# A two-layer fp32 trunk on one core: 32 bytes less padding ahead of the stages' pools, and steps of the attention plan in other places

## The chip, the cores and the metric

The kernel runs on one core of one Trainium2 chip. The metric is device time in microseconds (us), the median of three runs. A profile of one further execution gives a span (first to last instruction) and the trace that is read here. Engines: PE is TensorE's matmul, PEld its weight load, DVE is VectorE, ACT is ScalarE, POOL is GpSimd, SP issues DMAs.

## The reference, cut to what matters

512 positions, width 1024, two layers. Each layer is x + mixer(rmsnorm(x)) and then x + conv_ffn(rmsnorm(x)). The FFN is `(gelu(causal_dwconv(u)) * v) @ w_down` with `u, v = split(h @ w_up)` and 2816 hidden columns. The first layer's mixer is a causal pooling and a gated short convolution. The second layer's is the gated linear attention that the change touches:

```
q, k, v, r, gl = split(hn @ gla_w_in)
g    = log_sigmoid(gl @ w_g2 + b_g) / 16           # per head: cumulative sum bcum in chunks of 64
q_in = q * 128**-0.5 * exp(bcum);  k_in = k * exp(-bcum)
att  = where(tril, q_in @ k_in.T, 0);  kv = (k * exp(b_last - bcum)).T @ v
o    = att @ v + q_in @ states                     # states: decayed sum of kv over chunks
o    = o * rsqrt(mean(o*o) + eps) * norm_g * silu(r);   y = o @ gla_w_out
```

There are 4 heads, with 128 key columns and 256 value columns each.

## The kernel before, in words

All activations lie in SBUF transposed: 128 channels on partitions, 512 tokens along the free axis. A fp32 product is made of three fp32r matmuls: every operand is split into a high part (an ACT copy to fp32r, `high`) and a low part (a DVE subtraction, `low`), and high x high, high x low and low x high are summed in PSUM.

The large projections (w_up and the later part of w_down in both FFNs, and the query/key weights of the attention) are done by a seven-product scheme (`seven_weights`, line 473; `seven_product`, line 548): seven products p1 to p7 of 12 matmuls with 256 moving columns stand in for eight. There are 21 of them in each FFN's up part, 4 in each down part, and 4 in the attention (one for each head): 54 in all. A seven needs the weight parts a1, s31p, s2 and a2. Three of them have 1024 columns and lie in the ring `wsp` (tiles of `WPITCH` = 1088 columns, names `hi` and `lo`). s2 has 512 columns, serves product p6 alone, and lies in the pool of the stage (tiles of 576 columns, names `sh` and `sl`, line 509). All of them are put 19 columns (`SKEW`) into their tile. In the attention the products come in the order p1 p2 p6 p5 p7 p3 p4. p6, p7 and p4 go to the same PSUM bank as p1, one after another, so each must wait until an ACT copy (`keep`, line 1306) has fetched what stood there. p3 and p4 use a2.

Pools are opened in the order cp, big, wp, wsp, hp, sp and, last, the pool of the stage (`open_stage`: side, up, dn, up, gla and so on, one at a time); they lie in SBUF one behind another in this order. sp holds small tiles, each rounded up to 32 bytes a partition, and one tile "gap" that is never used (line 149). In the program's addresses cp to hp end at byte 201,600, a multiple of 128. sp takes 2,336 bytes, and every stage pool begins at byte 203,936, which is 32 past a multiple of 128. The `hi` and `lo` tiles begin at multiples of 128, and so do the activations (`xh`, `xl`, `th`, `tl`) that stream past the weights; the pitch of the `sh` and `sl` tiles (2,304 bytes) is a multiple of 128 too. In the stage dn the first three of the fourteen pairs `mh`, `ml` of the hidden activations that w_down's plain products stream lie in the stage's pool (`split_m`), the others in big.

The attention is written as a plan. `at(t, fn)` notes a step with a due time in us, `then` adds a PE step and moves the time on, and `run_plan` issues all steps in order of due time. On PE, DVE and ACT that order is kept as it stands, so an instruction waits for all that is planned ahead of it on its engine. DMAs go out on SP and POOL as their tiles come free. For each of four heads the plan has: a gate block r (`gate`, 24 matmuls of 512 columns, from a weight block whose high and low parts are due `split_at` us before it), the seven of query and key (`queries_keys`), three exponentials on ACT (`gates_of`: `decays2` makes exp(-b), line 1044; `decays` on DVE the difference and `decays3` the other two, lines 1048 and 1049), the keys on DVE (`head_keys`), `head_scores` (masked scores, and `key_rows` that copies the transposed keys), `head_kv` and `states`, `head_out`, the squares and the norm (`squares_of`, `head_norm`: two matmuls L311 and L312 need the ACT copy L315 and the DVE subtraction L316), and `out_gate` (times silu(r), and the split for the output projection `go`). Gate blocks 4 to 7 come after the fourth seven, and the last heads' pieces are put between their three parts.

Of the kernel before, what the change touches and what calls it, by code (L numbers as in the profile page):

```python
# [7 lines left out]
F32 = mybir.dt.float32  # L8
# [5 lines left out]
P = 128  # L14
# [58 lines left out]
def trunk_kernel(ctx, tc, xT, cols, w_ab, w_pool, w_abo, w_vg, w_qk, w_r, w_g2, w_go, w_up, w_dn, w_ds, outT):  # L73
# [72 lines left out]
    V.memset(ones, 1.0)  # L146
    ones_r = cp.tile([P, P], F32R, tag="ones_r", name="ones_r")
    V.tensor_copy(ones_r, ones)
    sp.tile([P, 56], F32, tag="gap", name="gap", bufs=1)
    warm_in = sp.tile([P, 1], F32, tag="warm", name="warm_in", bufs=1)  # L150
    S.activation(warm_in, ones[:, 0:1], AF.Abs_reciprocal_sqrt)
    warm = ps.tile([P, T], F32, tag="ps", name="warm")
# [306 lines left out]
    def at(t, fn):  # L459
        events.append((t, len(events), fn))  # L460
# [24 lines left out]
    def seven_weights(src, base, pool, sums, behind=None):  # L485
        w = {}

        def load_sum():
            s31 = w["s31"] = stage[pool].tile([P, WBLK], F32, tag="sum", name="s31", bufs=sums)
            part = src[:, None, D : D + QUARTER].broadcast_to([P, 2, QUARTER])  # L490
            nc.sync.dma_start(s31.rearrange("p (a n) -> p a n", a=2), part)

        def add_sum():
            part = src.rearrange("p (a n) -> p a n", a=4)[:, 0:4:3, :]
            G.dma_start(w["s31"].rearrange("p (a n) -> p a n", a=2), part, accum_op=ALU.add)  # L495

        def load_left():
            w["raw", 0] = wp.tile([P, WBLK], F32, tag="raw", name="raw")
            nc.sync.dma_start(w["raw", 0], src[:, :D])

        def load_right():
            w["raw", 1] = wp.tile([P, WBLK], F32, tag="raw", name="raw")
            nc.sync.dma_start(w["raw", 1][:, QUARTER:], src[:, D + QUARTER :])

        def tiles(kind, wide):
            if wide:
                return wsp.tile([P, WPITCH], F32R, tag=kind, name=kind)[:, SKEW : SKEW + WBLK]
            tag, bufs = "s" + kind[0], 2 if pool == "up" else 1
            return stage[pool].tile([P, T + 64], F32R, tag=tag, name=tag, bufs=bufs)[:, SKEW : SKEW + T]

        def high(name, src, wide=True):
            h = tiles("hi", wide)
            S.activation(h, src(), AF.Copy)  # L513
            w[name] = (h, src)

        def low(name, wide=True):
            h, src = w[name]
            lo = tiles("lo", wide)
            V.tensor_tensor(lo, src(), f32(h), ALU.subtract)  # L519
            w[name] = (h, lo)  # L520

        def s2_sum():
            s2 = w["raw", 1][:, :QUARTER]
            V.scalar_tensor_tensor(
                s2, w["s31"][:, QUARTER:], -1.0, w["raw", 0][:, :QUARTER], ALU.mult, ALU.subtract
            )

        def s4_sum():
            s2 = w["raw", 1][:, :QUARTER]
            V.tensor_tensor(s2, w["raw", 0][:, QUARTER:], s2, ALU.subtract)  # L530

        def queued_sum():
            with tc.issue_after(behind):
                load_sum()

        at(base - 26.0, queued_sum if behind else load_sum)
        at(base - 20.0, add_sum)
        at(base - 15.4, load_left)
        at(base - 9.7, load_right)
        at(base - 6.75, lambda: high("a1", lambda: w["raw", 0]))  # L540
        at(base - 4.35, lambda: low("a1"))
        at(base - 2.7, lambda: high("s31p", lambda: w["s31"]))
        at(base - 2.4, s2_sum)
        at(base - 1.65, lambda: high("s2", lambda: w["raw", 1][:, :QUARTER], False))
        at(base - 0.95, lambda: low("s2", False))
        at(base - 0.3, s4_sum)
        at(base + (0.4 if pool == "up" else 1.55), lambda: high("a2", lambda: w["raw", 1]))
        at(base + 1.5, lambda: low("s31p"))
        at(base + 3.3, lambda: low("a2"))

        return w

# [333 lines left out]
    rs, norm = norm_wide(acc, D)  # L886
# [155 lines left out]
    def decays2(h):  # L1042
        enb = heads[h]["enb"] = slot(name="enb")
        S.activation(enb, heads[h]["bc"], AF.Exp, scale=-1.0 / 16.0)
# [115 lines left out]
    def squares_of(h, t):  # L1160
        q = heads[h]

        def raw():
            q["sq"] = [slot(name="osq") for _ in range(2)]
            for sq, o in zip(q["sq"], q["o"]):
                S.activation(sq, o, AF.Square)

        def total():
            V.tensor_tensor(q["sq"][0], q["sq"][0], q["sq"][1], ALU.add)
            q["ro"], q["norm"] = norm_wide(q["sq"][0], 256, "ro")  # L1170

        at(t, raw)
        at(t + 1.3, total)
        ready_at = 6.5 if h < 2 else 1.7
        at(t + ready_at, lambda: q["norm"][0]())
        at(t + ready_at + 0.6, lambda: q["norm"][1]())

    def out_norm(h, t):
        q = heads[h]
# [10 lines left out]
    def out_gate(h, e, t):  # L1190
        i = 2 * h + e

        def gate():
            y = heads[h]["y"][e]
            V.tensor_tensor(y, y, sil[i], ALU.mult)

        def high():
            y_h[i] = slot(F32R, "yh")
            S.activation(y_h[i], heads[h]["y"][e], AF.Copy)

        def low():
            y_l[i] = slot(F32R, "yl")
            V.tensor_tensor(y_l[i], heads[h]["y"][e], f32(y_h[i]), ALU.subtract)

        at(t, gate)
        at(t + 0.8, high)
        at(t + 1.5, low)
# [12 lines left out]
    t = 0.0  # L1220
# [117 lines left out]
    def gate(i, between={}, split_at=(6.0, 4.8)):  # L1338
        project_into("r", i, store_r, between, split_at)
        at(t + 1.2, lambda: S.activation(sil[i], sil[i], AF.Silu))  # L1340
        sil_at[i] = t + 1.8
# [10 lines left out]
    def head_kv(h):  # L1352
        then(1.0, lambda: kv(h))
        at(t + 0.1, lambda: states(h))

    def head_out(h):
        then(3.1, lambda: outputs(h))
        squares_of(h, t + 0.1)

    def head_norm(h):  # L1360
        then(0.46, lambda: heads[h]["norm"][2]())
        out_norm(h, t + 0.1)
        scaled_at[h] = t + 5.4

    def gates_of(h, t):
        at(t + 2.0, lambda: decays(h))
        at(t + 3.0, lambda: decays2(h))
        at(t + 5.8, lambda: decays3(h))

    gate(0)  # L1370
    gates_of(0, t)
    queries_keys(0)
    head_keys(0, 1.6)
    gate(1, split_at=(4.6, 3.4))
    head_scores(0)
    gates_of(1, t)
    queries_keys(1)
    head_kv(0)
    head_keys(1, 1.6)
    gate(2, split_at=(4.6, 3.4))  # L1380
    head_out(0)
    head_scores(1)
    gates_of(2, t)
# [1 line left out]
    head_norm(0)  # L1385
    head_kv(1)
    head_keys(2, 1.6)
    gate(3, split_at=(4.6, 3.4))
    head_out(1)
    head_scores(2)  # L1390
    gates_of(3, t)
# [2 lines left out]
    head_norm(1)  # L1394
    head_kv(2)
    head_keys(3, 1.6)
    gate(4, split_at=(4.6, 3.4))
    head_out(2)
    head_scores(3)
    gate(5, {1: lambda: head_norm(2)})  # L1400
    head_kv(3)
    gate(6, {1: lambda: head_out(3)})
    gate(7, {1: lambda: head_norm(3)})
    for h in range(HEADS):
        for e in range(2):
            out_gate(h, e, max(scaled_at[h] + 0.7 * e, sil_at[2 * h + e], late + 10.0 * h + 0.7 * e if h < 2 else 0.0))
    for i in range(2):
        block(t - 8.0 + 3 * i, t - 5.0 + 2.5 * i, t - 3.8 + 2.5 * i)
    run_plan()
# [141 lines left out]
```

## Time and profile before

| | us |
|---|---|
| median of 3 runs (range) | 1017.31 (1017.26 to 1017.68) |
| the profiled execution: its own time | 1017.95 |
| its span | 1016.3 |
| PE busy | 1004.1 (99%) |
| DVE busy | 848.0 (83%) |
| ACT busy | 622.9 (61%) |
| mean granted TensorE clock | 0.996 of full speed |

In a timeline a row is a run of equal instructions: start, time from the first's start to the last's end, engine, line, operation, output <- inputs, count, and in brackets the idle time ahead of it with what ended it. Matmuls overlap, so the pace of PE is read from the differences between starts, not from the durations. The query/key products of head 0 begin at 524.86 us, those of head 3 at 585.64 us.

### The profile page before, as it was taken

What the parts mean: (1) busy time and instruction counts of PE and PEld (TensorE: products, weight loads), DVE (VectorE), ACT (ScalarE), POOL (GpSimd) and SP (SyncE); (2) the same over time, 40 slices, a digit from 0 to 9 for tenths busy, and PEclk for the clock granted to TensorE, in tenths of its full rate; (3) what the DMA queues carried; (4) which work ended last, traced back from release to release, by engine and by line L of the source; (5) the groups of instructions that cost most, each with busy time, mean ns of one, the idle gap of its engine ahead of it and who ended that gap; (6) DMA issues with size and microseconds to landing.
All of it is one profiled execution on the core that took longest, in us unless ns stands there. A gap on an engine that the chain in (4) does not pass through costs nothing.

```text
span 1016.3 us, 17534 instructions
## 1 busy us (share of the span) xinstructions
PE 1004.1 (99%) x6996; PEld 931.3 (92%) x6996; DVE 848.0 (83%) x1224; ACT 622.9 (61%) x954; POOL 69.6 (7%) x93
## 2 busy tenths in 40 slices
PE   9999999999999999999999999999999999999996
PEld 7888889999999988899999998889999999988896
DVE  7886689999999997767777788889999999997775
ACT  6442567676666754345775668767676666754451
POOL 0001000111111000002000000100110110000000
PEclk9999999999999999999999999999999999999998
DMA  6437137778787455527235122737778777454522
GB/s 226 153 92 185 56 102 186 181 196 191 187 203 183 132 129 143 129 76 203 90 96 132 53 63 84 194 107 192 172 199 187 194 199 191 127 130 131 130 83 84
DMA packets 61267, 147.03 MB, mean 145 GB/s; under 512 B 5152, under 2 KB 7584, under 8 KB 61184
## 3 DMA queue, kind: packets, MB, share of 16 engines
q1 hardware_dynamic: 45808, 116.93, 37.3%
q0 software_dynamic: 14688, 28.32, 17.1%
q8 instruction: 55, 0.90, 0.4%
q10 hardware_dynamic: 688, 0.65, 0.2%
q14 instruction: 28, 0.23, 0.1%
HBM read 143.78 MB, written 2.10 MB: 144 GB/s over the span
## 4 chain that ended last, share of the span: by engine, by line
PE 92%; DVE 4%; ACT 3%; issue 1%; DMA 1%; SPq 0%; DVEq 0%; ACTq 0%
PE stx L562 29%; PE styz L562 18%; PE dn L264 15%; PE go L264 4%; PE abo L264 4%; PE r L1274 3%; PE pc L264 2%; PE pb L264 2%; PE px L264 2%; PE dn L562 2%; PE stz L562 1%; PE v L596 1%; PE u L596 1%; PE pu L264 1%; PE vg L1065 1%
## 5 line engine op out<-in xcount | busy, mean ns | idle before, releaser
L519 DVE TENSOR_TENSOR lo<-raw,hi 128x1024 fp32r<-128x1024 f32 x108 | 131.7, 1220 | 12.9 <-ACT hi L513 12.9
L513 ACT ACTIVATE hi<-raw 128x1024 fp32r<-128x1024 f32 x108 | 114.1, 1057 | 21.5 <-PE styz L562 18.2
L223 DVE TENSOR_TENSOR lo<-raw,hi 128x1024 fp32r<-128x1024 f32 (+3 forms) x83 | 95.8, 1156 | 10.4 <-ACT hi L219 9.7
L219 ACT ACTIVATE hi<-raw 128x1024 fp32r<-128x1024 f32 (+3 forms) x83 | 83.1, 1001 | 19.2 <-PE pc L264 5.1
L495 POOL DMA_DIRECT2D s<-in_w_up x42 | 50.6, 1205 | 577.6 <-ACT k L614 102.3
L380 DVE SCALAR_TENSOR_TENSOR cacc<-u,colt,cacc 128x511 f32<-128x511 f32 x96 | 71.5, 745 | 1.8 <-ACT cacc L377 1.8
L377 ACT ACTIVATE cacc<-u,colt 128x512 f32<-128x512 f32 x48 | 39.2, 817 | 45.0 <-DVE u L629 35.9
L519 DVE TENSOR_TENSOR lo<-s,hi 128x1024 fp32r<-128x1024 f32 x54 | 65.7, 1216 | 0.0
L513 ACT ACTIVATE hi<-s 128x1024 fp32r<-128x1024 f32 x54 | 57.3, 1062 | 4.4
L562 PE MATMUL stx<-th,hi 128*128 128x256 f32 x368 | 56.9, 276 | 0.8 <-ACT q L1306 0.8
L264 PE MATMUL dn<-mh,hi 128*128 128x512 f32 (+1 forms) x238 | 57.0, 379 | 0.0
L264 PE MATMUL dn<-ml,hi 128*128 128x512 f32 (+1 forms) x238 | 56.9, 378 | 0.0
L264 PE MATMUL dn<-mh,lo 128*128 128x512 f32 (+1 forms) x238 | 56.8, 378 | 0.0
L562 PE MATMUL stx<-th,lo 128*128 128x256 f32 x368 | 56.8, 276 | 0.0
L562 PE MATMUL stx<-tl,hi 128*128 128x256 f32 x368 | 56.7, 276 | 0.0
L562 PE MATMUL styz<-xh,hi 128*128 128x256 f32 x360 | 55.8, 277 | 0.0
L562 PE MATMUL styz<-xh,lo 128*128 128x256 f32 x360 | 55.5, 276 | 0.0
L562 PE MATMUL styz<-xl,hi 128*128 128x256 f32 x360 | 55.4, 276 | 0.0
L264 PEld LDWEIGHTS dn<-mh,lo 128*128 128x128 f32 x238 | 43.0, 188 | 8.6
L264 PEld LDWEIGHTS dn<-ml,hi 128*128 128x128 f32 x238 | 43.0, 188 | 8.6
L264 PEld LDWEIGHTS dn<-mh,hi 128*128 128x128 f32 x238 | 42.3, 188 | 8.1
L562 PEld LDWEIGHTS stx<-th,hi 128*128 128x128 f32 x368 | 48.6, 188 | 1.0 <-ACT q L1306 1.0
(347 smaller groups left out, 2607.4 us busy)
## 6 DMA issues: line engine op xcount, KB each, us to landing
raw<-in_w_up SPq DMA_DIRECT2D x46, 512.0 KB, 6.0
s<-in_w_up SPq DMA_DIRECT2D x42, 512.0 KB, 6.8
s<-in_w_up POOLq DMA_DIRECT2D x42, 512.0 KB, 6.5
raw<-in_w_dn SPq DMA_DIRECT2D x32, 448.0 KB, 3.4
raw<-in_w_up SPq DMA_DIRECT2D x42, 256.0 KB, 3.3
raw<-in_w_ab SPq DMA_DIRECT2D x14, 512.0 KB, 3.7
raw<-in_w_abo SPq DMA_DIRECT2D x8, 512.0 KB, 4.1
s<-in_w_ds SPq DMA_DIRECT2D x8, 512.0 KB, 6.5
```

The source lines that it names most:

```text
L219: S.activation(parts[0], raw, AF.Copy)
L223: V.tensor_tensor(parts[1], raw, f32(parts[0]), ALU.subtract)
L264: PE.matmul(out, w[:, k, :], a[k], start=first and i == 0 and k == 0, stop=last and i == 2 and k == n - 1, skip_group_check=loose,)
L377: S.activation(acc[0], u, AF.Identity, bias=col(bname, j), scale=col(wname, 2 * nj + j))
L380: V.scalar_tensor_tensor(a, u[:, : T - i], col(wname, (2 - i) * nj + j), a, ALU.mult, ALU.add)
L495: G.dma_start(w["s31"].rearrange("p (a n) -> p a n", a=2), part, accum_op=ALU.add)
L513: S.activation(h, src(), AF.Copy)
L519: V.tensor_tensor(lo, src(), f32(h), ALU.subtract)
L562: PE.matmul(b[out][:, ts], wt[:, ks[k]], a[k], start=first and i == 0 and k == 0, stop=i == 2 and k == HK - 1, skip_group_check=True,)
L596: PE.matmul(o, w[:, k, :], a[k], start=i == 0 and k == 0, stop=i == 2 and k == KD - 1)
L1065: PE.matmul(o[c][:, :n], xh[kk][:, cs], lo[:, k, :], start=False, stop=kk == KD - 1)
L1274: PE.matmul(o, w[:, k, :], a[k], start=i == 0 and k == 0, stop=i == 2 and k == KD - 1, skip_group_check=True)
```

## The change

Every edit, with nothing left out:

```diff
-    sp.tile([P, 56], F32, tag="gap", name="gap", bufs=1)
+    sp.tile([P, 48], F32, tag="gap", name="gap", bufs=1)
...
-        at(base + (0.4 if pool == "up" else 1.55), lambda: high("a2", lambda: w["raw", 1]))
+        at(base + {"up": 0.4, "gla": 4.4}.get(pool, 1.55), lambda: high("a2", lambda: w["raw", 1]))
         at(base + 1.5, lambda: low("s31p"))
-        at(base + 3.3, lambda: low("a2"))
+        at(base + (5.3 if pool == "gla" else 3.3), lambda: low("a2"))
...
-        at(t + ready_at + 0.6, lambda: q["norm"][1]())
+        at(t + ready_at + (1.6 if h < 2 else 0.6), lambda: q["norm"][1]())
...
-        at(t + 3.0, lambda: decays2(h))
+        at(t + 1.6, lambda: decays2(h))
...
-    gate(1, split_at=(4.6, 3.4))
+    gate(1, split_at=(3.6, 2.4))          # gate(2), gate(3) and gate(4) alike
...
-    gate(5, {1: lambda: head_norm(2)})
-    head_kv(3)
-    gate(6, {1: lambda: head_out(3)})
+    gate(5, {1: lambda: (head_kv(3), head_norm(2))})
+    gate(6, {0: lambda: head_out(3)})
...
-            out_gate(h, e, max(scaled_at[h] + 0.7 * e, sil_at[2 * h + e], late + 10.0 * h + 0.7 * e if h < 2 else 0.0))
+            out_gate(h, e, max(scaled_at[h] + 0.7 * e, sil_at[2 * h + e], late + 5.0 + 8.0 * h + 0.7 * e if h < 2 else 0.0))
```

The gap tile has 8 columns fewer, so all that lies behind it, the stages' pools above all, moves down by 32 bytes: they begin at byte 203,904, a multiple of 128. In the attention, `high("a2")` is due 2.85 us later and `low("a2")` 2.0 us later; `decays2` comes 1.4 us earlier (in the order of ACT it passes from behind `high("a2")` to ahead of it); the DVE step of the norm of heads 0 and 1 and the split of the gate blocks 1 to 4 come 1.0 us later; `head_kv(3)` passes from behind gate block 5 into it, ahead of `head_norm(2)`; `head_out(3)` goes one third of gate block 6 earlier; the output gating of head 0 is due 5 us later and that of head 1 3 us later. No instruction is added or removed.

## Rows read from the trace of the kernel before

**Rows 1.** The page's first part: busy time, share of the span, instructions.

```profile
PE 1004.1 (99%) x6996; PEld 931.3 (92%) x6996; DVE 848.0 (83%) x1224; ACT 622.9 (61%) x954; POOL 69.6 (7%) x93
```

**Rows 2.** The waits of PE in the attention: line, what it waited for, us in total, times, longest.

```profile
PE stx L562 <- ACT q L1306: 0.8, 1, 0.8
...
PE ss L312 <- DVE nl L316: 0.2, 1, 0.2
```

**Rows 3.** Groups of PE's instructions with shapes kept apart, whole span: count | busy us, mean ns of one | idle before.

```profile
L562 PE MATMUL stx<-th,hi 128*128 128x256 f32 x368 | 56.9, 276 | 0.8 <-ACT q L1306 0.8
...
L562 PE MATMUL stx<-tl,sh 128*128 128x256 f32 x184 | 29.8, 285 | 0.0
L562 PE MATMUL stx<-th,sl 128*128 128x256 f32 x184 | 29.4, 283 | 0.0
...
L562 PE MATMUL stx<-xl,sh 128*128 128x256 f32 x32 | 5.2, 285 | 0.0
...
L264 PE MATMUL dn<-ml,hi 128*128 128x256 f32 x28 | 4.0, 282 | 0.0
```

**Rows 4.** PE's timeline in the first FFN's up part: p6 begins at 164.09, the next product at 165.52, the one after it at 166.89.

```profile
164.09 0.64 PE L562 MATMUL stx<-th,sh 128*128 128x256 f32 x4
...
165.52 0.63 PE L562 MATMUL styz<-xh,hi 128*128 128x256 f32 x4
...
166.89 0.62 PE L562 MATMUL styz<-th,hi 128*128 128x256 f32 x4
```

**Rows 5.** The chain of work that ended last, in order of time: start, us, what.

```profile
98.06 43.52 PE abo L264 x192
...
355.02 38.42 PE dn L264 x168
393.44 1.38 PE stx L562 x12
396.18 1.44 PE stx L562 x12
```

**Rows 6.** Stretches: us, then PE busy (instructions), PEld, DVE, ACT, POOL, PE's clock, DMA share, GB/s; four sevens in the first FFN's up part.

```profile
201.15:239.59 38.44, 38.44 (x339) 38.44 (x338) 36.13 (x50) 26.37 (x41) 4.80 (x4) 1.00 0.79 192
```

**Rows 7.** ACT's timeline in head 3: `keep` of q's first half, the high part of a2, the table load and exponential of `decays2`, `keep` of q's second half.

```profile
587.30 0.39 ACT L1306 ACTIVATE q<-stx 128x256 f32<-128x256 f32 x1
588.91 1.06 ACT L513 ACTIVATE hi<-raw 128x1024 fp32r<-128x1024 f32 x1 [1.23 <-DVE raw L530]
589.99 1.28 ACT L1044 ACT_TABLE_LOAD   x1
591.28 0.63 ACT L1044 ACTIVATE enb<-bc 128x512 f32<-128x512 f32 x1
591.82 0.37 ACT L1306 ACTIVATE q<-stx 128x256 f32<-128x256 f32 x1
```

**Rows 8.** PE's timeline in head 3: the last third of p6, the last third of p5, the first of p7.

```profile
589.42 0.64 PE L562 MATMUL stx<-th,sl 128*128 128x256 f32 x4
...
590.81 0.64 PE L562 MATMUL stz<-th,lo 128*128 128x256 f32 x4
592.24 0.73 PE L562 MATMUL stx<-th,hi 128*128 128x256 f32 x4 [0.78 <-ACT q L1306]
```

**Rows 9.** DVE's timeline in head 3: the low part of a2.

```profile
591.19 1.21 DVE L519 TENSOR_TENSOR lo<-raw,hi 128x1024 fp32r<-128x1024 f32 x1
```

**Rows 10.** ACT's timeline in head 0: `keep` of q's second half, the high part of gate block 1, the two exponentials of `decays3`, `keep` of k's second half.

```profile
529.62 0.37 ACT L1306 ACTIVATE q<-stx 128x256 f32<-128x256 f32 x1
529.88 1.05 ACT L219 ACTIVATE hi<-raw 128x1024 fp32r<-128x1024 f32 x1
530.83 0.62 ACT L1048 ACTIVATE bc<-bc 128x512 f32<-128x512 f32 x1
531.35 0.62 ACT L1049 ACTIVATE ek<-ek 128x512 f32<-128x512 f32 x1
531.96 0.39 ACT L1306 ACTIVATE k<-stx 128x256 f32<-128x256 f32 x1
```

**Rows 11.** PE's timeline in head 0: first and last third of p3, first of p4.

```profile
531.76 0.62 PE L562 MATMUL styz<-xh,hi 128*128 128x256 f32 x4
...
532.67 0.62 PE L562 MATMUL styz<-xh,lo 128*128 128x256 f32 x4
533.12 0.62 PE L562 MATMUL stx<-th,hi 128*128 128x256 f32 x4
```

**Rows 12.** PE's timeline in gate block 5: its second third, the two matmuls of head 2's norm.

```profile
610.83 1.98 PE L1274 MATMUL r<-xl,hi 128*128 128x512 f32 x8
612.64 0.40 PE L311 MATMUL ss<-nh,ones_r 128*128 128x512 f32 x1
613.21 0.50 PE L312 MATMUL ss<-nl,ones_r 128*128 128x512 f32 x1 [0.17 <-DVE nl L316]
```

**Rows 13.** ACT's timeline there: the transposed keys of head 3, which `head_kv(3)` needs.

```profile
612.34 0.47 ACT L1128 ACTIVATE kt<-kot 128x384 f32<-128x384 f32 x1
```

**Rows 14.** DVE's timeline there: the subtraction that L312 needs.

```profile
612.46 0.69 DVE L316 TENSOR_TENSOR nl<-osq,nh 128x512 fp32r<-128x512 f32 x1
```

**Rows 15.** SP's timeline: the load of the right weight part of head 1, which takes the buffer that the low part of head 0's a2 gives back.

```profile
529.06 0.33 SPq L503 DMA_DIRECT2D raw<-in_w_qk  x1
```

More of the change, by code (lines that the diff above doesn't have):

```diff
@@ L1379, in trunk_kernel @@
     head_keys(1, 1.6)
-    gate(2, split_at=(4.6, 3.4))
+    gate(2, split_at=(3.6, 2.4))
     head_out(0)
@@ L1387, in trunk_kernel @@
     head_keys(2, 1.6)
-    gate(3, split_at=(4.6, 3.4))
+    gate(3, split_at=(3.6, 2.4))
     head_out(1)
@@ L1396, in trunk_kernel @@
     head_keys(3, 1.6)
-    gate(4, split_at=(4.6, 3.4))
+    gate(4, split_at=(3.6, 2.4))
     head_out(2)
     head_scores(3)
-    gate(5, {1: lambda: head_norm(2)})
-    head_kv(3)
-    gate(6, {1: lambda: head_out(3)})
+    gate(5, {1: lambda: (head_kv(3), head_norm(2))})
+    gate(6, {0: lambda: head_out(3)})
     gate(7, {1: lambda: head_norm(3)})
```

## The prediction

> **What bounds the kernel now.** I read the page's busy times first: PE works 1004.1 us of the 1016.3 us span, 99%, DVE 83%, ACT 61% [rows 1]. PE is the bound nearly everywhere, so time can only come from two places: instants in which PE idles, and matmuls that take longer than they need. Second, PE's waits. In the attention, which the plan edits touch, there is one of 0.8 us on an ACT copy of q and one of 0.2 us on the norm's subtraction [rows 2]. All plan edits together can therefore win little over 1 us, and more only by accident. Third, I looked for slow matmuls with shapes kept apart. All fp32r matmuls with 256 moving columns last 276 ns, save those whose weights are the tiles `sh` and `sl`: 283 to 285 ns [rows 3]. The pace, read from the starts, says the same: a product with these weights takes 165.52 - 164.09 = 1.43 us, the next one 166.89 - 165.52 = 1.37 us [rows 4], and in the down part the chain gives 1.44 against 1.38 us [rows 5].
>
> Why should `sh` be slow? The same activations stream past `hi` and past `sh`, the shapes are equal, and the half of the weights, the bank and the neighbours change from product to product without effect. What is particular to `sh` and `sl` is where they lie. Both kinds are read from column 19, byte 76 of the tile; `hi` and `lo` tiles begin at a multiple of 128, the stage's tiles 32 bytes past one. So fast weights stand at 76 past a multiple of 128, slow ones at 108, under activations that stand at 0. One more group points the same way: in the last blocks of w_down the weights are at 76 too, but some of the activations `mh`, `ml` lie in the stage's pool at 32, and the group's mean is 282 ns, not 276 [rows 3]. The difference between the two addresses is then again 44 modulo 64. I read this as a price on the distance between weights and moving data.
>
> **The change part by part.** *Padding.* The stage pools move from 32 past to 0 past a multiple of 128. `sh` and `sl` then stand at 76, as `hi` does, and should run as fast. One p6 saves 1.43 - 1.36 = 0.07 us (1.36 is 12 matmuls from the start of p3, 531.76, to that of p4, 533.12 [rows 11]). There are 54 sevens: 54 x 0.07 = 3.8 us, all on PE's path. Bounds: 0 if the place is not the cause, and 54 x 0.08 = 4.3 us with the rounding of the starts. The saving needs DVE to follow: four sevens take 38.44 us, DVE is busy 36.13 of them [rows 6], 9.03 of 9.61 us a seven, so a seven of 9.54 us still leaves it half a microsecond.
>
> The `mh` and `ml` pairs in the stage's pool, three of fourteen, gain too. 168 matmuls of dn take 38.42 us, 228.7 ns each, where 192 of abo take 226.7 [rows 5]. If the place of three pairs made all of that, the 630 such matmuls of both layers would give back 1.3 us; the 84 short ones at the end up to 84 x 6 ns = 0.5 us. With 3/14 of the operands affected I take 0.2 us, bounds 0 and 1.8.
>
> Here the Trainium skill speaks against the edit. In "SBUF — State Buffer", section "SBUF: two separate sides", it says that within the engine side only the port pair shared by VectorE and GpSimd causes contention, and that TensorE never waits on anyone; its specifications give cachelines of 16 bytes as the unit in which a place matters, and 76 and 108 lie equally in those. By that rule a shift of 32 bytes would give nothing and the sum below would come to 1016.1 us. The pace of `sh` beside `hi` in this trace does not agree with it.
>
> *The three exponentials and a2.* In head 3 ACT does: q's first half at 587.30, the high part of a2 at 588.91 (it had waited for its input), the table load at 589.99, exp at 591.28, q's second half at 591.82 [rows 7]. PE needs that last copy before p7, because p7 overwrites the bank. p5's last third starts at 590.81, and thirds follow each other after 0.45 us; p7 could start at 591.26 and starts at 592.24 [rows 8]: 0.97 us lost. After the change the load and exp stand ahead of the high part of a2: load at 587.7, exp until 589.6; p6 ends at 589.42 + 0.64 = 590.06, q's copy then runs to 590.4, before 591.26. The stall goes: -0.97 us.
>
> What is late next? The high part of a2 now follows the copy: 590.35 to 591.4, the low part (1.21 us [rows 9]) ends at 592.6. p3 needs the high part when it starts, 591.26 + 1.36 = 592.6, and the low part in its last third, 0.9 us later. 0.9 us to spare at either place. Head 0 is the tightest, because there the high part of gate block 1 also stays ahead of the copy of k's second half, which p4 waits for. p4 starts at 533.12 [rows 11], so p6 ends three products earlier, at 529.2 with its tail. The steps of that queue [rows 10] then start at: copy of q 529.2, high a2 529.46, exps 530.41 and 530.93, high of gate block 531.45, copy of k 532.40, done 532.79. p4 would start at 533.05: 0.26 us to spare, where it had 0.77. In heads 1 to 3 the copy of k stands ahead of the gate block. I take 0 for new stalls here, bounds 0 and 4 x 0.3 us. The number of table loads doesn't change: between silu and the last exponential only copies move.
>
> The low part of a2 gives its buffer back later, and SP loads head 1's right weight part into it: issued at 529.06 before [rows 15], about 531.8 after. The plan puts 7.3 us between that load (base - 9.7) and its first use (base - 2.4), so 4.6 us are left. Behind it on SP stands the load of gate block 2, which is due 14 us later still. I take 0, bounds 0 and 1 us. The later split of the gate blocks (1 us, needed at the block's first and last third) and the later subtraction of norms 0 and 1 are covered by the same queues; if they weren't, gate blocks would wait on PE, at most 1 us each.
>
> *Gating and the last heads' pieces.* PE issues L311 at 612.64, L312 at 613.21, where the pace for 512 columns is 0.227 us [rows 5]: 0.34 us lost to the subtraction, 612.46 + 0.69 = 613.15 [rows 12, 14]. After the change `head_kv(3)` (1.1 us) stands there, and the norm comes after it, when the subtraction is done. But `head_kv(3)` needs the transposed keys, whose copy ends at 612.34 + 0.47 = 612.81 [rows 13], 0.2 us after PE is ready for it. PE would be ready at 610.83 + 8 x 0.227 = 612.65. ACT's queue ahead of that copy changes twice: the two copies of head 0's gating come in, and waits on DVE go out. I take half of the 0.2 us. Gain 0.34, new wait 0.1: -0.2 us, bounds -0.4 and +1.0. `head_out(3)` one third earlier needs head 3's states, but these come earlier as well: they are due 4.0 us ahead of it in the plan (139.3 and 143.3), before 3.5 us. The gating moved back leaves DVE free for head 3's keys; its last step is due at 140.2, and `go` begins at 155.9. Cost 0, and up to 0.5 us if the states are late.
>
> Sum, against the profiled execution: 1017.95 - 3.8 - 0.2 - 0.97 - 0.2 = 1012.8 us. The median of the runs is 0.64 us under that execution, so **1012.1 us**.
>
> **The rivals.** *The padding works, the plan gives nothing or costs.* For it: ACT's order is tight in head 0, and one slip in a queue that is kept in order moves everything behind it. Against: 0.9 us to spare in the other heads. Without the plan's 1.2 us: 1013.3; with a new stall of 1 us on top, 1014.3.
>
> *Place doesn't matter.* Something else about `sh` would slow it, its short pitch for instance. For it: the trace has no tile of the same name at another distance. The rule named above is this case. Against: the slow group at the end of w_down. Then only the plan is left: 1017.31 - 1.2 = 1016.1, within what can't be told from no change.
>
> *The a2 chain becomes the wait.* Place: the last third of p3 in each attention head, behind copy, high and low of a2. It decides from 0.9 us of delay on; a delay d costs 4 x (d - 0.9). If the padding gave nothing as well, d = 2.2 us would make 1016.1 + 5.2 = 1021.3. For it: three engines wait in a row there. Against: nothing in the queues shown [rows 7 to 11] delays the copy by 2 us once the exponential has gone ahead.
>
> **How the numbers follow.** A measurement of this kernel tells 0.2%, about 2 us, from no change. Both parts as worked out: 0.75, between 1011.0 and 1013.0 (upper bound of the stage's terms below, a stall of 0.9 above). Padding alone: 0.15, 1013.0 to 1014.6. Place doesn't matter: 0.06. The a2 chain: 0.04. Faster by over 0.2% (under 1015.3) are the first two: 0.90; same 0.06; slower 0.04. The range runs from 1010.8 to 1013.9: the first case, with the lower end for the w_down term at more than I take, and about half of the second.
>
> **What would show it.** The groups with `sh` and `sl` should read 276 ns, a seven in the up part 9.54 us between starts of the same product, and the last short group of dn 276 to 278. PE's waits should no longer have the copy of q nor L312, and p7 of head 3 should start 0.45 us after the last third of p5. Wrong would be `sh` still at 283 to 285 (the place is not the cause), new waits of PE on the low part of a2 or the copy of k (the plan), or DVE as the releaser of PE in the up part.

## The result and the profile after

| | before | after |
|---|---|---|
| median (range), us | 1017.49 (1017.26 to 1017.68), 4 runs | 1011.45 (1010.77 to 1011.80), 4 runs |
| profiled execution: own time, span | 1017.95, 1016.3 | 1011.80, 1010.1 |

The ratio is 0.994, 95% interval 0.9923 to 0.9957. 1012.1 us had been forecast, with a range of 1010.8 to 1013.9; the result lies 0.65 us below the forecast. The parts behind the sum differ more than the sum does.

The page's first part, of the kernel after; beside [rows 1] PE is 5.8 us shorter, DVE and ACT do the same as before.

```profile
PE 998.3 (99%) x6996; PEld 926.1 (92%) x6996; DVE 846.6 (84%) x1224; ACT 622.3 (62%) x954; POOL 69.5 (7%) x93
```

PE's waits in the kernel after, whole span: us in total, times, longest.

```profile
PE vg L1065 <- DVE lo L223: 0.7, 2, 0.4
...
PE ss L312 <- DVE nl L316: 0.2, 1, 0.2
```

The wait for ACT's copy of q [rows 2] is gone. That for the norm stands there as before, with the same 0.2, and it is another one: the timeline below puts it at head 3's norm, not at head 2's. A list of waits by line hides such an exchange.

PE's groups with shapes apart, kernel after: count | busy us, mean ns of one | idle before.

```profile
L562 PE MATMUL stx<-th,hi 128*128 128x256 f32 x368 | 56.8, 276 | 0.0
...
L562 PE MATMUL stx<-th,sl 128*128 128x256 f32 x184 | 28.4, 276 | 0.0
L562 PE MATMUL stx<-tl,sh 128*128 128x256 f32 x184 | 28.4, 276 | 0.0
...
L562 PE MATMUL stx<-xl,sh 128*128 128x256 f32 x32 | 4.9, 276 | 0.0
...
L264 PE MATMUL dn<-ml,hi 128*128 128x256 f32 x28 | 3.9, 280 | 0.0
```

All groups with `sh` and `sl` now read 276 ns, as `hi` does [rows 3]; the last group of w_down fell from 282 to 280 only. The chain of waits, kernel after, in order of time; the first two lines answer to [rows 5].

```profile
98.05 43.52 PE abo L264 x192
...
353.17 38.10 PE dn L264 x168
...
539.28 1.44 PE stx L562 x12
...
545.04 1.44 PE stx L562 x12
```

The last two are p1 and p7 of head 1. The same chain in the kernel before, p6 and p7 of head 1:

```profile
544.94 1.44 PE stx L562 x12
...
547.75 1.36 PE stx L562 x12
```

Two things are to be seen. 168 matmuls of dn take 38.10 us, 226.8 ns each, now at the pace of abo (226.7); before they took 228.7. And in head 1 of the attention, products of 12 matmuls last 1.44 us though their weights, all but those of p6, stand where they always stood. Before, only p6 was so slow there.

To place gains and losses I cut the span by starts read from PE's timelines: FFN 0 from the first abo matmul to the last row of dn; heads from p1 of head 0 to p1 of head 3; seven 3 from there to the transposition L1118 of head 3's keys; tail from there to the first matmul of `go`; rest from `go` to the end of the span. The experiments below are in the same table.

| us | FFN 0 | heads | seven 3 | tail | rest | span |
|---|---|---|---|---|---|---|
| before | 370.78 | 60.78 | 23.03 | 22.64 | 384.99 | 1016.3 |
| after | 367.96 | 61.03 | 21.85 | 22.97 | 382.20 | 1010.1 |
| e1_pad | 367.97 | 61.03 | 23.00 | 22.58 | 381.59 | 1010.4 |
| e2_plan | 370.76 | 60.77 | 21.86 | 23.02 | 384.44 | 1014.8 |
| e3_small_weights | 368.60 | 60.52 | 22.99 | 22.61 | 382.30 | 1011.7 |
| e8_no_tail | 367.95 | 61.03 | 21.86 | 22.58 | 381.95 | 1009.4 |
| e9_no_exp | 367.95 | 61.03 | 23.04 | 23.01 | 381.98 | 1010.5 |
| e10_gap32_same_place | 368.66 | 60.77 | 21.84 | 22.98 | 382.51 | 1011.6 |
| e11_gla_lead | 367.98 | 60.49 | 21.88 | 22.64 | 381.75 | 1009.4 |
| e12_norm2_later | 367.96 | 60.50 | 21.86 | 22.72 | 382.14 | 1009.4 |

The first four columns agree within some 0.05 us among kernels that should agree there. The rest differs by up to 0.6 us, and the span holds, besides, the start (the first abo matmul comes at 97.31 to 98.46 us) and the stretch ahead of head 0 (0.2 us), so small effects are read from the first four. The change gave -2.82 (FFN 0), +0.25 (heads), -1.18 (seven 3), +0.33 (tail) and -2.79 us (rest): -6.2 us together.

### The profile page after: what moved, and what is told of

It is laid out like the page before. It is cut to its first block, busy times and chain, and to the rows that moved or that the text cites. A ratio compares the mean times of both kernels' runs of the same rounds, so it can differ in the third digit from the quotient of the medians.

```text
span 1010.1 us, 17534 instructions
## 1 busy us (share of the span) xinstructions
PE 998.3 (99%) x6996; PEld 926.1 (92%) x6996; DVE 846.6 (84%) x1224; ACT 622.3 (62%) x954; POOL 69.5 (7%) x93
## 4 chain that ended last, share of the span: by engine, by line
PE 92%; DVE 3%; ACT 3%; DMA 1%; issue 0%; SPq 0%; DVEq 0%; ACTq 0%
PE stx L562 29%; PE styz L562 18%; PE dn L264 15%; PE go L264 4%; PE abo L264 4%; PE r L1274 2%; PE pc L264 2%; PE dn L562 2%; PE px L264 2%; PE pb L264 2%; PE stz L562 2%; PE v L596 1%; PE u L596 1%; PE pu L264 1%; DVE lo L223 1%; PE vg L1065 1%
## 5 line engine op out<-in xcount | busy, mean ns | idle before, releaser
L513 ACT ACTIVATE sh<-raw 128x512 fp32r<-128x512 f32 x54 | 34.2, 634 | 24.6 <-DVE raw L524 24.6
```

## The experiments

Edits are shown against the kernel after unless it is said otherwise.

**The two halves alone.** e1_pad is the kernel before with the padding edit alone. e2_plan is the kernel after without it.

```diff
-    sp.tile([P, 56], F32, tag="gap", name="gap", bufs=1)      # e1_pad, against before
+    sp.tile([P, 48], F32, tag="gap", name="gap", bufs=1)
-    sp.tile([P, 48], F32, tag="gap", name="gap", bufs=1)      # e2_plan, against after
+    sp.tile([P, 56], F32, tag="gap", name="gap", bufs=1)
```

> The kernel before with only the padding smaller (56 to 48 columns). Theory of the prediction: 4.0 us come from the padding, 1013.5, the rest of the 6.0 us that were measured from the plan. Theory from the traces: the plan's stall at head 3 is gone but three smaller new waits took its place, so the plan is worth some 0.5 us and the padding some 5.5: 1012.0. In either case `sh` and `sl` at 276 ns.

> The changed kernel with the padding of before (48 back to 56 columns). Theory of the prediction: 1017.5 - 1.2 = 1016.3. Theory from the traces: 1017.5 - 0.5 = 1017.0. `sh` and `sl` at 283 to 285 ns, and in the down part the matmuls of the plain blocks slower where the streamed operand changes between stage pool and big.

e1_pad: 1012.4 us, ratio 0.9946 (0.9933 to 0.9959). e2_plan: 1017.13 us, ratio 0.9993 (0.9984 to 1.0003). Padding makes nearly all of it. By the table the plan is worth 0.8 us in the attention with either padding (heads, seven 3 and tail sum to 106.45 before and 105.65 in e2_plan, to 106.61 in e1_pad and 105.85 after). Whole runs can hardly show that. The table also shows that padding alone lengthens the heads, by 0.25 us.

**Weights without the rest of the stage.** In e3_small_weights, made from the kernel before, the pools stay at 32 and only the s2 parts move, to 32 + 44 = 76 past a multiple of 128.

```diff
-            return stage[pool].tile([P, T + 64], F32R, tag=tag, name=tag, bufs=bufs)[:, SKEW : SKEW + T]
+            return stage[pool].tile([P, T + 64], F32R, tag=tag, name=tag, bufs=bufs)[:, 11 : 11 + T]
```

> The kernel before, with the parts of s2 put at column 11 instead of 19 of their tiles, so that they stand at 32 + 44 = 76 past a multiple of 128 while the pool stays where it was. If the place of the weights is the cause, `sh` and `sl` read 276 ns and 54 products save 0.072 us each, 3.9 us: 1013.6. If something else of the stage's pool slows them, 1017.5. What e1 wins beyond this run is owed to the other tiles of the stages' pools; theory: about 1.3 us, from `mh` and `ml` in dn.

1012.83 us, ratio 0.9953 (0.994 to 0.9966), 0.8 us under what was expected, since a seven gave more than the 0.072 us taken. PE's groups with shapes apart:

```profile
L264 PE MATMUL dn<-mh,hi 128*128 128x512 f32 x210 | 53.1, 392 | 0.0
...
L562 PE MATMUL stx<-tl,sh 128*128 128x256 f32 x184 | 28.3, 276 | 0.0
...
L264 PE MATMUL dn<-ml,hi 128*128 128x256 f32 x28 | 4.0, 282 | 0.0
```

`sh` is at 276 ns while dn keeps its old 392 and 282 ns. That separates the two gains of the padding. FFN 0 loses 370.78 - 368.60 = 2.18 us by s2 (25 sevens, 0.087 each) and 368.60 - 367.96 = 0.64 us by dn. It also excludes the pitch of the `sh` tiles as the reason, since the tiles are the same.

**What about the place?** The prediction had guessed that weights cost more when their distance from the moving data is 44 modulo 64. In e4_cp48 the padding of cp grows by 32 bytes: all weights stand at 108, `th`, `tl` and `mh` at 32, while `xh` and `xl`, which lie ahead of that padding, stay at 0.

```diff
-    cp.tile([P, 40], F32, tag="gap", name="gap")
+    cp.tile([P, 48], F32, tag="gap", name="gap")
```

> The changed kernel with 32 bytes more padding in the pool cp, behind xh and xl: all later pools move up by 32, so all weights of the sevens stand at 108, the streamed th, tl, bh, bl at 32, and xh, xl stay at 0. If the distance between weights and streamed data counts, only the products that stream xh and xl become slow (2040 matmuls x 6 ns = 12.2 us): 1023.7; with th, tl they stay at 276 ns. If the place of the weights alone counts, all 4536 become slow: 1038.7. If neither, 1011.5.

1035.09 us, ratio 1.017 (1.0155 to 1.0184). PE's groups with shapes apart:

```profile
L562 PE MATMUL styz<-xl,hi 128*128 128x256 f32 x360 | 58.8, 286 | 0.0
...
L562 PE MATMUL stx<-th,hi 128*128 128x256 f32 x368 | 57.9, 279 | 0.0
...
L562 PE MATMUL stx<-tl,sh 128*128 128x256 f32 x184 | 28.4, 276 | 0.0
...
L562 PE MATMUL stx<-xl,sh 128*128 128x256 f32 x32 | 5.2, 287 | 0.0
```

The same weights at 108 are slow with `xl` at 0 (286, 287 ns) and fast, or fast after a start, with `th`, `tl` at 32 (276 to 279 ns). So the place of the moving data counts too, and 108 as such is no slow place. The whole cost lies between what distance alone (1023.7 us) and the place of the weights alone (1038.7 us) had made it: slower products cost up to 11 ns a matmul, and the `th` group that reads 279 ns costs something too.

In e5_sweep the s2 parts of the 42 sevens of both up parts are read from columns 0 to 41, one column further each time. In e6_gap40 and e7_gap32 the gap tile has 40 and 32 columns, so s2 stands at 44 and at 12 past a multiple of 128.

```diff
+        off = SKEW                      # e5_sweep, in seven_weights; ups = [0] ahead of it
+        if pool == "up":
+            off = ups[0]
+            ups[0] += 1
...
-            return stage[pool].tile([P, T + 64], F32R, tag=tag, name=tag, bufs=bufs)[:, SKEW : SKEW + T]
+            return stage[pool].tile([P, T + 64], F32R, tag=tag, name=tag, bufs=bufs)[:, off : off + T]
```

> The changed kernel with the parts of s2 of the 42 sevens of the up parts at columns 0, 1, 2 ... 41 of their tiles, one column further in each seven; the streamed data stay at 0. The pace of each p6 gives the price for its distance, in steps of 4 bytes. Theory: 1.36 us at column 19 (76 bytes) and 1.43 us at column 27 (108) and column 11 (44), a pattern that repeats after 16 columns (64 bytes). Rival: it repeats after 32 columns, so that column 11 is fast.

> The changed kernel with the padding 32 bytes smaller again: the stages' pools begin 96 past a multiple of 128, `sh` at 172. If the pattern repeats after 64 bytes, this is as slow as before the padding: `sh` at 283 to 285 ns, 1011.5 + 5.4 = 1016.9. If any smaller padding helps, or it repeats after 128, 1011.5.

> The changed kernel with the padding 64 bytes smaller than before the last step (32 columns): the stages' pools begin 64 past a multiple of 128. If the pattern repeats after 64 bytes, it is as fast as the changed kernel, `sh` at 276 ns, 1011.5; if after 128, slow.

e5_sweep 1018.0 us (one run), e6_gap40 1030.15 us (ratio 1.013, 1.0113 to 1.0146), e7_gap32 1039.01 us (one run). From the starts in e5_sweep a matmul of p6 takes 113 ns at 64, 76 and 88 past a multiple of 128, and 115 to 122 ns at all other places. "44 modulo 64" falls: 44 and 108 are slow as it has it, but so are 12, which it would put with 76, and nearly all other places. What holds is weaker: fast where s2 stands with the other weights, slow nearly everywhere else, with two exceptions (64, 88) that I can't explain. After p6 at 12, 44, 48, 52, 56 and 100 the other products behind it, whose addresses are unchanged, run at 120 ns as well, until a p6 at 16, 60 or 104 ends it; 48, 52 and 56 came while the pace was slow already, so they are only seen to keep it. At the remaining places they are back at 113 ns after one product at most. The place alone doesn't decide it: 12 came once more in the second FFN, and there the products behind it were fast.

e6_gap40 came out 13 us above the slower of its two expectations, and it says the same more plainly. s2 stands at 44 in all its sevens, yet in the up parts the products behind p6 are slow in one seven and fast in the next, in strict turn through all 42. PE's timeline there, the first two products behind p6 in two successive sevens:

```profile
166.19 0.62 PE L562 MATMUL styz<-xh,hi 128*128 128x256 f32 x4
...
167.55 0.62 PE L562 MATMUL styz<-th,hi 128*128 128x256 f32 x4
...
175.77 0.64 PE L562 MATMUL styz<-xh,hi 128*128 128x256 f32 x4
...
177.21 0.64 PE L562 MATMUL styz<-th,hi 128*128 128x256 f32 x4
```

They follow each other after 1.36 us in the one and 1.44 us in the other. So the place modulo 128 alone is not the rule. The up pools hold two buffers of each s2 tile, which are used in turn; a p6 at 44 could also turn over the pace that it meets. In this run the two always go together, and they were not separated.

PE's groups with shapes apart, of e7_gap32, where s2 is at 12 in all sevens:

```profile
L562 PE MATMUL stx<-th,hi 128*128 128x256 f32 x368 | 59.1, 283 | 0.0
...
L562 PE MATMUL stx<-th,sl 128*128 128x256 f32 x184 | 29.1, 279 | 0.0
```

Here the untouched `hi` is slower than `sl` whose place is wrong. The slow products behind p6 account for the large totals, but the pool moved as well; e10_gap32_same_place takes e7_gap32 and puts s2 back to 64 + 12 = 76.

```diff
-    sp.tile([P, 48], F32, tag="gap", name="gap", bufs=1)
+    sp.tile([P, 32], F32, tag="gap", name="gap", bufs=1)
...
-            return stage[pool].tile([P, T + 64], F32R, tag=tag, name=tag, bufs=bufs)[:, SKEW : SKEW + T]
+            return stage[pool].tile([P, T + 64], F32R, tag=tag, name=tag, bufs=bufs)[:, 3 : 3 + T]
```

> The kernel after with 16 columns less of the gap tile (the stages' pools at 64 past a multiple of 128, as in e7_gap32, which took 1039.0 us) and the s2 parts read from column 3 of their tiles in place of 19, so that they stand at 64 + 12 = 76 again, as the other weights do. Theory A (the place of the s2 weights against the other weights alone made all sevens slow in e7_gap32): sh, sl and hi groups of 256 columns all at 276 ns, only the dn products that stream mh, ml from the stage's pool at 64 change places: 1011.5 to 1013.2 us. Rival B (the place of the stage's pool, or the state of the chip in that run, made them slow): hi groups at 282 to 283 ns again and 1035 us or more.

1013.31 us (one run), with the signs of theory A and 0.1 us above its range. PE's groups with shapes apart:

```profile
L562 PE MATMUL stx<-th,hi 128*128 128x256 f32 x368 | 56.7, 276 | 0.0
...
L264 PE MATMUL dn<-mh,hi 128*128 128x512 f32 x210 | 53.0, 391 | 0.0
...
L562 PE MATMUL stx<-th,sl 128*128 128x256 f32 x184 | 28.4, 276 | 0.0
...
L264 PE MATMUL dn<-ml,hi 128*128 128x256 f32 x28 | 4.0, 283 | 0.0
```

Some 26 us of e7_gap32, between two single runs, hang on the place of the s2 weights alone. With the pool at 64 dn is slow again (391, 283 ns; FFN 0 0.70 us over after), as with the pool at 32. dn is at its best only where the three pairs of `mh`, `ml` in the stage's pool have the same place as the eleven in big.

**The parts of the plan.** e8_no_tail puts the last heads' pieces and the gating back, e9_no_exp the a2 parts, `decays2` and the splits.

```diff
-    gate(5, {1: lambda: (head_kv(3), head_norm(2))})            # e8_no_tail
-    gate(6, {0: lambda: head_out(3)})
+    gate(5, {1: lambda: head_norm(2)})
+    head_kv(3)
+    gate(6, {1: lambda: head_out(3)})
...                                                              # and late + 10.0 * h in out_gate
-        at(t + 1.6, lambda: decays2(h))                         # e9_no_exp
+        at(t + 3.0, lambda: decays2(h))
...                                                              # a2 at 1.55 and 3.3, split_at=(4.6, 3.4)
```

> The kernel after with the last heads' pieces and the gating put back (head_kv(3) behind gate block 5, head_out(3) a third later, gating due as before); padding, a2, exponentials and splits as after. Theory A (these edits brought three waits, 0.27 us on the copy of the transposed keys, 0.19 us on L312 of head 2's norm, 0.40 us on head 3's norm, and removed one of 0.34 us): all three go, the one comes back, the span falls by 0.5 us to 1009.6 us, the median to 1010.9. Rival B (the edits gain as predicted, 0.2 us or more, and head 3's late norm comes from the earlier a2 and exponentials): L312 of head 2 waits 0.34 us again, head 3's norm still waits 0.4 us, the span rises to 1010.4 or more.

> The kernel after with a2, the exponential of decays2 and the gate blocks' splits due as before; padding and the last heads' pieces as after. Theory A (these edits alone remove the stall of PE on q's copy): p7 of head 3 starts 1.4 to 1.5 us after the last third of p5 again, in place of 0.56, so the span rises by 0.9 us to 1011.0, the median to 1012.3; the waits on the keys' copy and on head 3's norm stay. Rival B (the stall went because the shorter p6 and the earlier weight parts changed what ACT meets, or what comes ahead of head 3 on ACT): p7 starts 0.5 to 0.7 us after p5's last third, the span stays at 1010.1.

e8_no_tail 1011.17 us, ratio 0.9932 (0.9919 to 0.9944), span 1009.4; e9_no_exp 1013.0 us, ratio 0.9949 (0.9936 to 0.9963), span 1010.5. Theory A both times, e9's span within 0.5 us of what was expected. In the table the exponentials, a2 and the splits, which went back together, give 23.04 - 21.85 = 1.19 us (the later DVE step of norms 0 and 1 stayed in both kernels and was not run by itself), and the last heads' edits cost 22.97 - 22.58 = 0.39 us. PE's timeline in e9_no_exp has the stall before p7 of head 3 again:

```profile
589.08 0.73 PE L562 MATMUL stx<-th,hi 128*128 128x256 f32 x4 [0.78 <-ACT q L1306]
```

PE's timeline in the kernel after, gate blocks 5 to 7:

```profile
607.11 1.97 PE L1274 MATMUL r<-xl,hi 128*128 128x512 f32 x8
609.19 1.56 PE L1135 MATMUL kv<-vt,kt 128*128 128x256 f32 x6
610.40 0.58 PE L311 MATMUL ss<-nh,ones_r 128*128 128x512 f32 x1
610.82 0.39 PE L312 MATMUL ss<-nl,ones_r 128*128 128x512 f32 x1
...
625.10 0.40 PE L311 MATMUL ss<-nh,ones_r 128*128 128x512 f32 x1
625.73 0.50 PE L312 MATMUL ss<-nl,ones_r 128*128 128x512 f32 x1 [0.23 <-DVE nl L316]
```

and in e8_no_tail:

```profile
608.86 0.39 PE L311 MATMUL ss<-nh,ones_r 128*128 128x512 f32 x1
609.44 0.50 PE L312 MATMUL ss<-nl,ones_r 128*128 128x512 f32 x1 [0.19 <-DVE nl L316]
...
625.12 0.40 PE L311 MATMUL ss<-nh,ones_r 128*128 128x512 f32 x1
625.36 0.40 PE L312 MATMUL ss<-nl,ones_r 128*128 128x512 f32 x1
```

In the kernel after `kv` starts 609.19 - 607.11 - 8 x 0.227 = 0.26 us late, L312 of head 2 follows L311 after 0.42 in place of 0.24, and that of head 3 after 0.63. In e8_no_tail `kv` is no longer late and head 3's L312 is prompt; head 2's stall is back at its old size, 0.58 - 0.24 = 0.34 us. ACT's timeline in the kernel after shows what holds head 3's norm:

```profile
611.98 0.63 ACT L1199 ACTIVATE yh<-y 128x512 fp32r<-128x512 f32 x1 [1.89 <-DVE y L1195]
...
613.42 1.28 ACT L318 ACT_TABLE_LOAD   x1
...
624.32 0.63 ACT L315 ACTIVATE nh<-osq 128x512 fp32r<-128x512 f32 x1 [1.36 <-DVE osq L1169]
```

The gating that the change put later (`yh`, with a wait of 1.89 us on its product) stands ahead of the table load of head 2's norm, at 613.42 where e8_no_tail has it at 611.27. The rest of that norm, head 2's gating and DVE's squares of head 3 follow late: `nh` at 624.32, in e8_no_tail at 623.00. e8_no_tail took three edits back at once; that the gating made head 3's wait is read from this order and was not run by itself.

**Head 1, and a better kernel.** In every kernel with the attention's pool at 0, head 1's seven is slow. e11_gla_lead is e8_no_tail with that one pool back at 32 and its s2 at 76.

```diff
     open_stage("gla")
+    stage["gla"].tile([P, 8], F32, tag="lead", name="lead", bufs=1)
...
-            return stage[pool].tile([P, T + 64], F32R, tag=tag, name=tag, bufs=bufs)[:, SKEW : SKEW + T]
+            c = 11 if pool == "gla" else SKEW
+            return stage[pool].tile([P, T + 64], F32R, tag=tag, name=tag, bufs=bufs)[:, c : c + T]
```

> e8_no_tail with 32 bytes more ahead of the attention's stage alone (an unused tile of 8 columns first in that pool), so that its tiles lie at 32 past a multiple of 128 as in the kernel before, and its s2 parts read from column 11, so that they stand at 76 like all other weights. Every other stage pool stays at 0. Theory A (head 1's seven runs at 0.48 us a third in all kernels whose attention pool lies at 0, since the products ahead of it, with operands from that pool, leave the slow pace behind): the thirds of head 1 go to 0.453 us, its seven from 10.15 to 9.64 us, the span from 1009.4 to 1008.9, the median to 1010.7. Rival B (the shift of 8 columns in the padding ahead of all pools did it some other way, or it is head 1's s2 place that matters): head 1 stays at 10.15 us, the span at 1009.4.

1010.54 us, ratio 0.9926 (0.9914 to 0.9938). PE's timeline in head 1, second and third third of p1, kernel after:

```profile
539.60 0.64 PE L562 MATMUL stx<-xl,hi 128*128 128x256 f32 x4
540.08 0.64 PE L562 MATMUL stx<-xh,lo 128*128 128x256 f32 x4
```

and e11_gla_lead:

```profile
540.16 0.62 PE L563 MATMUL stx<-xl,hi 128*128 128x256 f32 x4
540.62 0.62 PE L563 MATMUL stx<-xh,lo 128*128 128x256 f32 x4
```

0.48 us a third after, 0.46 here; the heads column falls by 0.54 us, as theory A has it, and the median lies 0.2 us under the 1010.7 expected. The products are the same; only tiles of the attention's pool, which the scores and transpositions ahead of p1 use, have moved. In e10_gap32_same_place, with the pool at 64, head 1 enters slow too and becomes fast just behind p6, though all weights of that seven stand at 76. Which operand sets the pace that p1 meets wasn't tried. The span of e11_gla_lead did not fall below that of e8_no_tail (1009.4), so this part of theory A was missed in the profiled execution: the first abo matmul started 0.40 us later, 98.25 against 97.85, and from the last row of dn to head 0 it took 0.23 us more, 56.41 against 56.18, as it does in other kernels of the table too (56.38 in e1_pad).

e12_norm2_later moves head 2's norm behind gate block 5 on top of that.

```diff
-    gate(5, {1: lambda: head_norm(2)})          # against e11_gla_lead
+    gate(5)
+    head_norm(2, -0.4)                          # out_norm(h, t - 0.4) in place of t + 0.1
```

> e11_gla_lead with the norm of head 2 (L311 and L312) one third of gate block 5 later on PE, behind the block, and its later steps due 1.4 us later. Theory A (L312 waits 0.35 us for the subtraction in e8_no_tail, and ACT's steps behind it wait for the table load of 611.3 us anyway): that wait goes and no other comes, the span falls by 0.35 us below e11_gla_lead, to 1008.55 if theory A holds there. Rival B (the chain behind the norm, head 2's gating and with it head 3's squares and norm, moves 1.4 us later and PE waits at head 3's norm, which had 0.8 us to spare): the 0.35 us comes back there as a wait of 0.4 us or more, span as e11_gla_lead or above.

1011.03 us, ratio 0.9931 (0.9917 to 0.9944). Rival B: head 2's L312 no longer waits and head 3's does again, 0.72 us behind L311; the tail is 22.72 against 22.64 us. The wait only changes its head.

e11_gla_lead has the shortest attention: heads, seven 3 and tail sum to 105.01 us, against 105.85 after. Its median is the lowest too, though its interval overlaps that of the kernel after.

## Why the prediction was right, and where its terms were not

| term, us | forecast | measured | from |
|---|---|---|---|
| p6 with `sh`, `sl`, 54 sevens | -3.8 | -4.7 | e3_small_weights, 0.087 a seven |
| dn's operands in the stage's pool | -0.2 | -1.3 | FFN 0: 0.64, for two layers |
| ACT's stall in head 3 | -0.97 | -1.18 | seven 3 column |
| last heads' pieces | -0.2 | +0.4 | tail column, e8_no_tail |
| head 1's seven | 0 | +0.5 | heads column, e11_gla_lead |
| sum | -5.2 | -6.3 | (profiled executions: -6.15) |

That the result lies in the range is partly luck. The two padding terms were 2.0 us too small, and two costs that were not in the sum, the last heads' pieces and head 1, took 1.1 us of that back.

**Padding and p6: right, reason half wrong.** That the place of `sh` makes it slow, and not its pitch, is shown by e3_small_weights. The Trainium skill, "SBUF — State Buffer", section "SBUF: two separate sides", says that TensorE waits on no one. The prediction had worked out from it that a shift of 32 bytes would give nothing; 4.7 us for such a shift, and the 26 us between e7_gap32 and e10_gap32_same_place, do not agree with that. The formula put on it, 44 modulo 64, was read from two points and is wrong. The size, 4.7 us, lies outside the bounds of 0 to 4.3, because only p6 was counted: by PE's starts in FFN 0, 0.075 us a seven are its own, and 0.010 us more lie on the product behind it, visible in [rows 4] as 1.37 in place of 1.36. "All" was also too much for the groups at 276 ns: `stx<-bh,hi` reads 280 ns in both kernels, and the padding did not touch it.

**dn: the mis-sized term.** The step that failed is "With 3/14 of the operands affected I take 0.2 us". The row in hand said 228.7 against 226.7 ns for all dn matmuls [rows 5], 1.3 us if the place made all of it, and that is what it made: 226.8 ns after. Scaling by 3/14 counted the effect twice, since the mean over fourteen pairs already held it. PE's timeline before shows what the mean is made of, rows of seven matmuls in a block that streams the pairs 0 to 6, three of them from the stage's pool, and then in one that streams the pairs 7 to 13, all from big:

```profile
356.48 1.77 PE L264 MATMUL dn<-ml,hi 128*128 128x512 f32 x7
358.09 1.77 PE L264 MATMUL dn<-mh,lo 128*128 128x512 f32 x7
...
377.42 1.75 PE L264 MATMUL dn<-mh,lo 128*128 128x512 f32 x7
379.00 1.75 PE L264 MATMUL dn<-mh,hi 128*128 128x512 f32 x7
```

A mixed row takes 1.61 us, 230 ns a matmul; the others follow each other after 1.58 to 1.59 us, 227 ns a matmul. The last short group, by contrast, fell only from 282 to 280 ns; it was to come to 276 to 278. The remaining 4 ns are not the pool's.

**The a2 chain: right.** ACT's and PE's timelines in head 3, kernel after, against [rows 7, 8]:

```profile
585.17 1.28 ACT L1044 ACT_TABLE_LOAD   x1
586.46 0.63 ACT L1044 ACTIVATE enb<-bc 128x512 f32<-128x512 f32 x1
587.48 0.39 ACT L1306 ACTIVATE q<-stx 128x256 f32<-128x256 f32 x1 [0.39 <-PE stx L562]
587.76 1.05 ACT L513 ACTIVATE hi<-raw 128x1024 fp32r<-128x1024 f32 x1
```

```profile
588.19 0.72 PE L562 MATMUL stz<-th,lo 128*128 128x256 f32 x4
588.75 0.63 PE L562 MATMUL stx<-th,hi 128*128 128x256 f32 x4
```

q's copy now waits for PE and not PE for it; p7 comes 0.56 us behind p5's last third (0.45 forecast, 1.43 before). The gain is 0.2 us larger than the stall, since before, the first third of p7 and the thirds of p4 had also been slow (0.56 us, and 0.52, 0.48 and 0.47, in place of 0.45 to 0.46). The tight place named in head 0 held: k's copy ended at 529.94, p4 started at 530.23, 0.29 us to spare where 0.26 had been worked out. The rival of the a2 chain did not occur.

**The last heads' pieces: wrong.** Forecast were a gain of 0.34 and a new wait of 0.1; the wait on the keys' copy came at 0.26 us, more than the whole lateness of which half had been taken. L312 of head 2 kept 0.18 us of its stall. What the prediction didn't see was head 3's norm: "Cost 0, and up to 0.5 us if the states are late" asked about the states and about DVE, but the gating put later stood ahead of the table load of head 2's norm on ACT. The queue that a moved step enters was followed on one engine only.

**Head 1: not foreseen.** The padding was taken to move only what is slow towards fast. It also moved the attention's other tiles, and one seven of four became slow.

**The rivals.** "Place doesn't matter" is excluded. "Padding works, plan gives nothing" is close to what the runs can tell of the plan: 0.8 us by the timelines, and 0.9993 (0.9984 to 1.0003) as a ratio.

## What to carry to other kernels

When one group of matmuls is slower than its equals, compare the byte places of both operands, not the code; and test it by moving one operand inside its tile, as e3_small_weights does, since moving a pool moves everything in it. A mean over a group that mixes affected and unaffected members is already diluted: scale from it by the count of all, not by the share again. A step that is put later joins a queue on every engine that it uses; follow it on each, down to the next wait of the bound engine, because a stall taken away at one head came back at the next in two of these kernels.

## What the runs showed of the hardware beyond what was expected

- The stream of 256 columns has two steady paces here, 113.3 ns a matmul (1.36 us for 12) and 120 ns (1.44 us), at the same granted clock of 0.996 to 0.997 in all profiled executions. Shapes, engines' waits and the work itself are equal at both.
- The pace can outlast its cause: with s2 at 12, the products behind p6 run at 120 ns in every seven with addresses that give 113 ns elsewhere (e7_gap32 against e10_gap32_same_place), and head 1's whole seven does so in the kernel after. What starts and ends it is not settled. A product at another place ended it in e5_sweep; that equal places merely keep the pace that they meet is a reading of this, was not tested, and has head 1 of e10_gap32_same_place against it, where the slow pace ended with all weights at 76. e6_gap40, with the same place in every seven and the two paces in turn, shows that the place modulo 128 is not the whole rule.
- The streams of 512 columns in dn are slower where a row mixes operands at different places, 230 ns a matmul in the mixed rows and 2 ns on average over all (228.7 against 226.7). With the pool at 64 the groups are slow as with it at 32 (391 to 392 ns against 389 to 390). Of the 0.025 us that a mixed row takes longer, about half lies on its first and fourth matmul, where the place changes (232 and 234 ns between starts, against 227); the rest is spread over the others, and why is open.
